# The first stage of a hybrid decoder layer: ones products ahead of the input, a compact weight block spread on chip, and squares behind the splits

## The chip, the cores and the metric

The kernel runs on one core of one Trainium2 chip. The metric is the device time of one execution in microseconds (us); the median of three runs is compared. A second number, the span, is taken from one profiled execution: it runs from the first to the last instruction that the profiler recorded.

## The reference

One layer (`DEPTH = 1`) of a decoder trunk, batch 1, 512 tokens behind 16 meta tokens, so 528 positions of 1024 channels, all in float32:

```
h = concat(meta, x)                       # 528 x 1024
u = rmsnorm(h) * mix_norm_w
proj = u @ w_in                           # pool 1024 | z 2048 | xbc 4096 | dt 32 | gates 2048
y_pool = pool_mixer(proj.pool) @ w_pool_up
y_ssd  = mamba2(z, xbc, dt) @ w_ssd_out   # conv + silu, chunked SSD, gated group norm
h = h + (sigmoid(g0) * y_pool + sigmoid(g1) * y_ssd) @ w_o
h = h + relu(rmsnorm(h) @ w_ff1)**2 @ w_ff2
out = rmsnorm(h)[16:]
```

In the first stage three things are made from x: the 32 columns of dt (one for each head), the first columns of xbc, and the mean of the squares of each position, from which the norm's factor `rsb = 1/sqrt(mean + eps)` comes. The factor is applied after the products here, so that they need not wait for it.

## The kernel before, in words

**Split products.** TensorE multiplies in a rounded float32 format (FP32R). For accuracy every operand is split in two: `hi` is the value cast to FP32R, and `lo` is what is left. ScalarE (ACT) makes `hi`, VectorE (DVE) subtracts it to make `lo`, and a product is three passes: hi·hi (L140), lo of the data with hi of the weights (L141), and hi of the data with lo of the weights (L143). `proj_step` writes these three for one slice k of 128 input channels, for each of two column runs of a result; `proj` runs it over k = 0 to 7.

**Weights.** All weights lie in DRAM as blocks of 128 x 1024. A block is loaded into `raw` (3 buffers, L68, from the queue of SyncE), cast into `whi` (4 buffers, L69, ACT) and split into `wlo` (4 buffers, L70, DVE). A `whi` buffer comes free only when the products of the block four before it have read it. Block 0 is dt, block 1 the first B columns (the result `px0_16`), block 2 the C columns (`px0_24`), blocks 3 and 4 two x blocks (`px0_0`, `px0_1`), 5 and 6 the two z blocks (one result, `pz0`), 7 to 9 gates (`pgp`).

**First stage** (L172 to L194). dt has only 32 columns. Its block holds them four times side by side, so that each quarter of the 128 result rows has all heads, and each quarter is later used for another stretch of 128 tokens. For k = 0 to 7 the slice `xt[k]` is loaded (L179), ACT scales and casts it to `xh[k]` (L180), DVE makes `xl[k]` (L181), TensorE runs two `proj_step` (dt into `pdt`, B into `px0_16`, 12 products in all), and ACT squares `xt[k]` (L190 and L193) with DVE adding the squares up in `q` (L194; the squares have 2 buffers). The two weight blocks come in an early part of 256 columns (slices 0 and 1) and a late part of 768.

**Norm factor.** `q` is split (L200, L201), four products with a matrix of ones sum it over the partitions (L209, L210, result `pn`), ACT takes the root (L211) and DVE the reciprocal (L212): `rsb`.

**The rest of the first group.** `px0_24`, `px0_0`, `px0_1` and `pz0` follow on TensorE. The wide results have two PSUM buffers that are taken in turn: `px0_16`, `px0_24`, `px0_0`, `px0_1`, `pz0`. So `px0_0` may begin when `px0_16` has been copied out, and `pz0` when `px0_0` has. The copy is `first_raw` (L295, ACT) into `raw0` (2 buffers), followed by a multiplication with `rsb` (L296, DVE), the convolution (L279 on ACT, three taps L282 on DVE) and a SiLU (L284, ACT). A `raw0` buffer comes free when its convolution is done.

**What sets the order.** The program is written as one sequence; the framework schedules it and decides in which order each engine takes its instructions. Each engine then runs its own list strictly in order, with semaphores between engines. So a line that moves in the source may move instructions of other lines too, on every engine.

Of the kernel before, what the change touches and what calls it, by code (L numbers as in the profile page):

```python
# [9 lines left out]
F32 = mybir.dt.float32  # L10
F32R = mybir.dt.float32r
AF = mybir.ActivationFunctionType
ALU = mybir.AluOpType

P = 128
# [5 lines left out]
NK = D // P  # L21
G = 8
R = 4
HEADS = 32
# [7 lines left out]
OFF_DT = 7168  # L32
# [7 lines left out]
GATES_FIRST = 3  # L40
GATE_AT = {1: 3, 2: 4, 3: 5, 5: 6}
POOL_ORDER = (3, 2, 1, 0)


@with_exitstack
def kernel(ctx: ExitStack, tc, xT, x, w, vec, fnw, out):
    nc = tc.nc
    act, dve, pe, pool = nc.scalar, nc.vector, nc.tensor, nc.gpsimd
# [10 lines left out]
    def block_tiles():  # L59
        b = nblk[0]  # L60
        nblk[0] += 1
        return (b, wp.tile([P, 1024], F32, tag="raw", name=f"raw{b}", bufs=3),
                wp.tile([P, 1024], F32R, tag="whi", name=f"whi{b}"),
                wp.tile([P, 1024], F32R, tag="wlo", name=f"wlo{b}"))

    def block_part(t, c):
        b, raw, hi, lo = t
        nc.sync.dma_start(raw[:, c], w[b, :, c])  # L68
        act.copy(hi[:, c], raw[:, c])  # L69
        dve.tensor_tensor(lo[:, c], raw[:, c], hi[:, c].bitcast(F32), op=ALU.subtract)  # L70

    def block():
        t = block_tiles()
        block_part(t, slice(0, 1024))
        return t[2:]
# [17 lines left out]
    ones_r = const.tile([P, P], F32R, name="ones_r")  # L93
# [14 lines left out]
    def col(off, i, n=P):  # L108
        return vs[:n, off + i : off + i + 1]
# [20 lines left out]
    def psum2(name):  # L130
        return psa.tile([P, 1024], F32, tag="mm", name=name)

    def psum1(name):
        return psb.tile([P, 512], F32, tag="s", name=name)

    def proj_step(outs, k, wblk, rhs):

        wh, wl = (t[:, k * P : (k + 1) * P] for t in wblk)
        for o, c in outs:
            pe.matmul(o, wh, rhs[0][k][:, c], start=k == 0, stop=False)  # L140
            pe.matmul(o, wh, rhs[1][k][:, c], start=False, stop=False)  # L141
        for o, c in outs:
            pe.matmul(o, wl, rhs[0][k][:, c], start=False, stop=k == NK - 1)  # L143
# [5 lines left out]
    def wide(ps, skip=0):  # L149

        h = (L - skip) // 2
        runs = [(ps[:, 512 - h : 512], slice(skip, skip + h)),
                (ps[:, 512 : 512 + h], slice(skip + h, L))]
        return runs, ps[:, 512 - h : 512 + h]
# [11 lines left out]
    X, U = (xh, xl), (uh, ul)  # L166
# [3 lines left out]
    pdt = [psum1(f"pdt{i}") for i in range(2)]  # L170
    dt_runs = [(pdt[0][:, : NM + 256], slice(0, NM + 256)), (pdt[1][:, :256], slice(NM + 256, L))]
    pB = psum2("px0_16")  # L172
    runsB, viewB = wide(pB)
    wdt, wB = block_tiles(), block_tiles()
    early, late = slice(0, 256), slice(256, 1024)
    for k in range(NK):
        if k == 0:
            block_part(wdt, early)
        nc.sync.dma_start(xt[k], xT[:, k, :])  # L179
        act.activation(xh[k], xt[k], AF.Copy, scale=col(V_MIX, k))  # L180
        dve.scalar_tensor_tensor(xl[k], xt[k], col(V_MIX, k), xh[k].bitcast(F32),  # L181
                                 op0=ALU.mult, op1=ALU.subtract)
        if k < 2:
            block_part((wB, wdt)[k], (early, late)[k])
        if k == 1:
            block_part(wB, late)
        proj_step(dt_runs, k, wdt[2:], X)
        proj_step(runsB, k, wB[2:], X)
        if k == 0:
            act.activation(q, xt[k], AF.Square)  # L190
        else:
            s = pre.tile([P, L], F32, tag="sq", name=f"sq{k}", bufs=2)
            act.activation(s, xt[k], AF.Square)  # L193
            dve.tensor_tensor(q, q, s, op=ALU.add)  # L194
# [11 lines left out]
    for i in range(2):  # L206
        c = slice(i * HALF, (i + 1) * HALF)
# [37 lines left out]
    for c in (slice(0, P), slice(P, W)):  # L245
        n = c.stop - c.start
# [5 lines left out]
    for j, src in enumerate((dt, acs)):  # L252
# [6 lines left out]
              start=True, stop=True)  # L259
# [302 lines left out]
    def gate_ssd(d):  # L562
        ps = psum1(f"pgs{d}")
        proj(narrow(ps), block(), U)
        gt = gtp.tile([P, SEQ], F32, tag="gt", name=f"gs{d}")
        act.activation(gt, ps, AF.Sigmoid, bias=col(V_BG, NK + d))
        return gt

    wgb = block()
    pend = [pool_tile(2 * POOL_ORDER[0] + i) for i in range(2)]  # L570
    for n, gi in enumerate(POOL_ORDER):
        nxt = []
        if n < 3:
            nxt.append(pool_tile(2 * POOL_ORDER[n + 1]))
        if n == 0:
# [6 lines left out]
        if n < 3:  # L582
            nxt.append(pool_tile(2 * POOL_ORDER[n + 1] + 1))
        pend = nxt


    gts.append(gate_ssd(1))
    ks = [2 * gi + i for gi in POOL_ORDER for i in range(2)]
    for d in range(NK):
        ps = psum2(f"pup{d}")[:, :SEQ]  # L590
        wh, wl = block()
        for n, k in enumerate(ks):
            c = slice(k * P, (k + 1) * P)
# [8 lines left out]
    for d in range(NK):  # L602
# [8 lines left out]
        h = mgp.tile([P, SEQ], F32R, name=f"mh{d}")  # L611
# [17 lines left out]
    for half in range(2):  # L629
# [5 lines left out]
        for kk in range(4):  # L635
            wh, wl = block()
            for k2 in range(2):
                k = 2 * kk + k2
                c = slice(k2 * 512, (k2 + 1) * 512)
# [4 lines left out]
        c = slice(half * 512, (half + 1) * 512)  # L644
        for t in range(4):
            dve.tensor_tensor(ht[:, t, c], ht[:, t, c], pv[t], op=ALU.add)
        for kk in range(4):
            k = 4 * half + kk
# [179 lines left out]
    c = NC - 1  # L828
# [5 lines left out]
    for t in range(4):  # L834
        T, st = t // 2, slice((t % 2) * P, (t % 2 + 1) * P)
        n = 0
        for half in range(2):
            parts = [(0, 512)] if half == 0 or t < 3 else [(0, 256), (256, 256)]
            for a, m in parts:
# [4 lines left out]
                for k, seg in ((1, (A11, 3)[T]), (0, (A12, A22)[T])):  # L844
                    wh, wl = wq[k, half]
                    for p in range(2):
# [3 lines left out]
                        for lhs, rhs in ((hh, wh), (hh, wl), (hl, wh)):  # L850
                            pe.matmul(ps, lhs[:, p, seg, st], rhs[:, x0 : x0 + m], start=f and lhs is hh and rhs is wh,
                                      stop=i == 4 and lhs is hl, skip_group_check=True)
# [11 lines left out]
def _weight_blocks(i):  # L864

    w_in, w_g, w_up = i["w_in"][0], i["pool_w_group"][0], i["w_pool_up"][0]
    w_so, w_o, f1, f2 = i["w_ssd_out"][0], i["w_o"][0], i["w_ff1"][0], i["w_ff2"][0]
    blocks = []

    def cols(m, c):  # L870
        a = m[:, c : c + P]
        return a.reshape(NK, P, P).transpose(1, 0, 2).reshape(P, NK * P)

    def put(b):
        blocks.append(b)

    put(cols(np.tile(w_in[:, OFF_DT : OFF_DT + HEADS], (1, P // HEADS)), 0))

    def group(g, gate_d=None):
        for t in (16 + g, 24 + g, 2 * g, 2 * g + 1):  # L880
            put(cols(w_in, OFF_XBC + t * P))
        if gate_d is not None:
            gate(gate_d)
        for j in range(2):
            put(cols(w_in, OFF_Z + (2 * g + j) * P))

    def wg(b):
        put(w_g[2 * b : 2 * b + 2].reshape(2, 2, P, 256).transpose(2, 0, 1, 3).reshape(P, 1024))

    def gate(d):  # L890
        put(cols(w_in, OFF_GATE + d * P))

    def pieces(ks):

        u = [w_so[k * P : (k + 1) * P, d * P : (d + 1) * P] for d in range(NK) for k in ks]
        return [np.concatenate(u[j : j + NK], 1) for j in range(0, len(u), NK)]

    group(0)
    for d in range(GATES_FIRST):
        gate(d)  # L900
    for g in range(G - 1):
        if g == 4:
            for d in range(NK):
                put(cols(w_so[:D], d * P))
        group(g + 1, GATE_AT.get(g))
    blocks += pieces(range(8, 14))
    wg(POOL_ORDER[0] // 2)
    for t in range(2):
        put(cols(w_in, (2 * POOL_ORDER[0] + t) * P))
    for n in range(4):  # L910
        if n < 3:
            put(cols(w_in, 2 * POOL_ORDER[n + 1] * P))
        if n == 0:
            gate(NK - 1)
        if n == 3:
            gate(NK)
        if n == 2:
            wg(POOL_ORDER[n] // 2)
        if n < 3:
            put(cols(w_in, (2 * POOL_ORDER[n + 1] + 1) * P))  # L920
    gate(NK + 1)
    for d in range(NK):
        put(cols(w_up, d * P))
    last = pieces((14, 15))
    for d in range(NK):
        if d + 2 < NK:
            gate(NK + d + 2)
        if d % 4 == 0:
            put(last[d // 4])

    def rows(m, k2, half):
        a = m[k2 * 2 * P : (k2 + 1) * 2 * P, half * 512 : (half + 1) * 512]
        return a.reshape(2, P, 512).transpose(1, 0, 2).reshape(P, 1024)

    for half in range(2):
        for kk in range(4):
            put(rows(w_o, kk, half))

    def quarter(c, k, half):

        a = [f2[(4 * c + 2 * p + k) * P : (4 * c + 2 * p + k + 1) * P, half * 512 : (half + 1) * 512]
             for p in range(2)]
        return np.concatenate(a, 1)

    def quarters(c):
        for k, half in ((1, 0), (1, 1), (0, 1), (0, 0)):
            put(quarter(c, k, half))

    ff = list(range(32))

    def ff1():
        if ff:
            put(cols(f1, ff.pop(0) * P))

    for _ in range(6):
        ff1()
    for c in range(8):
        quarters(c)
        for _ in range(3 if c > 4 else 4):
            ff1()  # L960
    return np.ascontiguousarray(np.stack(blocks))
# [38 lines left out]
```

## Time and profile before

| | us |
|---|---|
| median of three runs | 1034.2 (1033.74 to 1035.4) |
| the profiled execution, its own time | 1033.66 |
| its span | 1031.9 |
| TensorE (PE) busy | 1017.8, 99% |
| VectorE (DVE) busy | 714.5, 69% |
| ScalarE (ACT) busy | 542.5, 53% |

The span is 1.8 us shorter than the execution's own time. Times within the trace count from the span's start. A row of the timeline gives the start, the duration, the engine, the line, the operation with output and inputs, the shape and, in brackets, how long the engine was idle before it and what ended that. "x2" merges neighbours of one kind. PE durations are modelled to the end of the pipeline, so that neighbours overlap: the distance of two starts is the rate.

### The profile page before, as it was taken

To read this page: it belongs to the slowest core of one execution; us is meant where nothing else is said; L and a number is where in the kernel's file an instruction comes from. 1 tells how busy PE (TensorE), PEld (TensorE's weight loads), DVE (VectorE), ACT (ScalarE), POOL (GpSimd) and SP (SyncE) were. 2 spreads that over 40 slices of the span, in tenths; PEclk is the share of its full clock that TensorE was granted. 3 is DMA by queue.
4 is the path that set the end of the run, shared out by engine and by line. 5 is a ranking of instruction groups with operands and counts; after the bars stand their busy time and mean duration, and the time that the engine had idled before them with its cause. 6 is when DMAs were issued, how large, how long until landed. Compare 5 with 4: busy or idle time off the path is not lost.

```text
span 1031.9 us, 13993 instructions
## 1 busy us (share of the span) xinstructions
PE 1017.8 (99%) x5700; PEld 880.1 (85%) x5700; DVE 714.5 (69%) x932; ACT 542.5 (53%) x706; POOL 10.0 (1%) x24
## 2 busy tenths in 40 slices
PE   7999999999999999999999999999999999999997
PEld 7889989998889898988998888878888888888886
DVE  7978788687637586887674345645686676776866
ACT  8675968586627348573443223344554355454444
POOL 0100000000000000000000000000000000000000
PEclk9999999999999999999999999999999999999999
DMA  6333051413332321413232323543324323334112
GB/s 228 115 137 103 21 164 39 146 57 127 102 111 75 108 97 41 151 61 113 72 109 89 102 84 102 202 145 108 95 82 123 105 80 121 102 102 123 42 41 82
DMA packets 29424, 106.01 MB, mean 103 GB/s; under 512 B 3312, under 2 KB 4272, under 8 KB 28336
## 3 DMA queue, kind: packets, MB, share of 16 engines
q1 hardware_dynamic: 26640, 93.14, 28.6%
q0 software_dynamic: 2000, 11.08, 2.8%
q8 instruction: 45, 0.74, 0.3%
q10 hardware_dynamic: 720, 0.91, 0.2%
q14 instruction: 19, 0.16, 0.0%
HBM read 102.95 MB, written 2.16 MB: 102 GB/s over the span
## 4 chain that ended last, share of the span: by engine, by line
PE 97%; DVE 1%; DMA 1%; ACT 0%; issue 0%; SPq 0%; ACTq 0%
PE px L140 6%; PE px L141 6%; PE px L143 6%; PE pf L86 6%; PE pf L88 6%; PE pf L87 6%; PE alpha L744 3%; PE alpha L746 3%; PE alpha L745 3%; PE pz L140 3%; PE pz L141 3%; PE pz L143 3%; PE py L418 2%; PE pp L141 2%; PE pso L86 2%; PE pp L140 2%
## 5 line engine op out<-in xcount | busy, mean ns | idle before, releaser
L69 ACT CAST whi<-raw 128x1024 fp32r<-128x1024 f32 (+2 forms) x141 | 145.6, 1038 | 274.6 <-PE pf L87 61.2
L70 DVE TENSOR_TENSOR wlo<-raw,whi 128x1024 fp32r<-128x1024 f32 (+2 forms) x141 | 170.0, 1207 | 151.4 <-ACT whi L69 144.0
L140 PE MATMUL px<-uh,whi 128*128 128x264 f32 (+1 forms) x448 | 121.2, 290 | 0.7 <-DVE ct L282 0.7
L141 PE MATMUL px<-ul,whi 128*128 128x264 f32 (+1 forms) x448 | 118.9, 285 | 0.0
L86 PE MATMUL pf<-vh,whi 128*128 128x512 f32 x256 | 99.7, 389 | 1.2 <-DVE vl L653 1.2
L88 PE MATMUL pf<-vh,wlo 128*128 128x512 f32 x256 | 99.6, 389 | 0.0
L87 PE MATMUL pf<-vl,whi 128*128 128x512 f32 x256 | 99.6, 389 | 0.0
L143 PE MATMUL px<-uh,wlo 128*128 128x264 f32 (+1 forms) x448 | 90.8, 284 | 0.0
L140 PEld LDWEIGHTS px<-uh,whi 128*128 128x128 f32 x448 | 84.6, 189 | 2.8 <-issue 2.6
L141 PEld LDWEIGHTS px<-ul,whi 128*128 128x128 f32 x448 | 84.9, 189 | 0.3
L143 PEld LDWEIGHTS px<-uh,wlo 128*128 128x128 f32 x448 | 69.4, 188 | 0.3 <-issue 0.3
L695 DVE TENSOR_TENSOR slo<-b,shi 128x1024 fp32r<-128x1024 f32 x35 | 42.8, 1222 | 31.6 <-ACT shi L694 31.6
L694 ACT CAST shi<-b 128x1024 fp32r<-128x1024 f32 x35 | 36.8, 1051 | 51.8 <-PE pf L87 36.5
L86 PEld LDWEIGHTS pf<-vh,whi 128*128 128x128 f32 x256 | 48.0, 188 | 11.3 <-DVE vl L653 1.5
L88 PEld LDWEIGHTS pf<-vh,wlo 128*128 128x128 f32 x256 | 48.0, 188 | 10.1
L87 PEld LDWEIGHTS pf<-vl,whi 128*128 128x128 f32 x256 | 48.1, 188 | 10.0
L744 PE MATMUL alpha<-shi,hh 128*128 128x512 f32 x140 | 54.6, 390 | 0.0
L746 PE MATMUL alpha<-shi,hl 128*128 128x512 f32 x140 | 54.5, 389 | 0.0
L745 PE MATMUL alpha<-slo,hh 128*128 128x512 f32 x140 | 54.5, 389 | 0.0
L756 DVE TENSOR_TENSOR ht<-ht,alpha 128x1024 f32<-128x1024 f32 x35 | 42.6, 1218 | 6.1 <-PE alpha L746 6.1
L140 PE MATMUL pz<-uh,whi 128*128 128x512 f32 x112 | 44.0, 393 | 0.0
L141 PE MATMUL pz<-ul,whi 128*128 128x512 f32 x112 | 43.9, 392 | 0.0
(330 smaller groups left out, 2395.9 us busy)
## 6 DMA issues: line engine op xcount, KB each, us to landing
raw<-in_w SPq DMA_DIRECT2D x137, 512.0 KB, 3.6
b<-in_w SPq DMA_DIRECT2D x28, 512.0 KB, 3.6
abc<-acs_d POOLq DMA_DIRECT2D x8, 1024.0 KB, 7.2
xt<-in_xT SPq DMA_DIRECT2D x8, 264.0 KB, 6.2
ht<-in_x POOLq DMA_DIRECT2D x4, 512.0 KB, 5.8
w<-in_w SPq DMA_DIRECT2D x4, 512.0 KB, 3.5
out_dram<-out SPq DMA_DIRECT2D x4, 320.0 KB, 2.4
raw<-in_w SPq DMA_DIRECT2D x2, 384.0 KB, 5.5
```

Of the source, the lines that this page charges most:

```text
L69: act.copy(hi[:, c], raw[:, c])
L70: dve.tensor_tensor(lo[:, c], raw[:, c], hi[:, c].bitcast(F32), op=ALU.subtract)
L86: pe.matmul(ps, ah, bh, start=first, stop=False)
L87: pe.matmul(ps, ah, bl, start=False, stop=False)
L88: pe.matmul(ps, al, bh, start=False, stop=last)
L140: pe.matmul(o, wh, rhs[0][k][:, c], start=k == 0, stop=False)
L141: pe.matmul(o, wh, rhs[1][k][:, c], start=False, stop=False)
L143: pe.matmul(o, wl, rhs[0][k][:, c], start=False, stop=k == NK - 1)
L695: dve.tensor_tensor(lo, src, hi.bitcast(F32), op=ALU.subtract)
L744: pe.matmul(ps[t], a[0], wh[:, cs], start=f, stop=False, skip_group_check=True)
L745: pe.matmul(ps[t], a[0], wl[:, cs], start=False, stop=False, skip_group_check=True)
L746: pe.matmul(ps[t], a[1], wh[:, cs], start=False, stop=l, skip_group_check=True)
```

## The change

- Ahead of everything, TensorE runs 22 products of the 128 x 128 matrix of ones with itself into the buffer of `pdt[1]`, which the first real product overwrites.
- The dt block holds each weight once: 256 of its 1024 columns are used, [slice k][head]. They come in one load; ACT and DVE read them with a repeated (stride 0) access and write the four copies into `whi` and `wlo`, slices 0 and 1 first, the other six later. The late load of dt (768 columns) is gone.
- The loads stand in another order: `xt[2]` is asked for before the late part of block 1.
- The squares and their sums stand in a loop of their own, behind the splits and products of all eight slices.

```diff
+WARM = 22
...
     wdt, wB = block_tiles(), block_tiles()
-    early, late = slice(0, 256), slice(256, 1024)
-    for k in range(NK):
-        if k == 0:
-            block_part(wdt, early)
+    b, raw, hi, lo = wdt
+    nc.sync.dma_start(raw[:, :256], w[b, :, :256])
+    spread = lambda t: t.rearrange("p (k c h) -> p k c h", c=4, h=HEADS)
+    once = raw[:, :256].rearrange("p (k h) -> p k h", h=HEADS).unsqueeze(2).to_broadcast([P, NK, 4, HEADS])
+
+    for n in range(WARM):
+        pe.matmul(pdt[1][:, :P], ones_r, ones_r, start=True, stop=True)
+
+    def x_load(k):
         nc.sync.dma_start(xt[k], xT[:, k, :])
+
+    def x_split(k):
         act.activation(xh[k], xt[k], AF.Copy, scale=col(V_MIX, k))
         dve.scalar_tensor_tensor(xl[k], xt[k], col(V_MIX, k), xh[k].bitcast(F32),
                                  op0=ALU.mult, op1=ALU.subtract)
-        if k < 2:
-            block_part((wB, wdt)[k], (early, late)[k])
-        if k == 1:
-            block_part(wB, late)
+
+    x_load(0)
+    act.copy(spread(hi)[:, :2], once[:, :2])
+    dve.tensor_tensor(spread(lo)[:, :2], once[:, :2], spread(hi)[:, :2].bitcast(F32), op=ALU.subtract)
+    x_split(0)
+    block_part(wB, slice(0, 256))
+    x_load(1)
+    proj_step(dt_runs, 0, wdt[2:], X)
+    proj_step(runsB, 0, wB[2:], X)
+    x_split(1)
+    act.copy(spread(hi)[:, 2:], once[:, 2:])
+    dve.tensor_tensor(spread(lo)[:, 2:], once[:, 2:], spread(hi)[:, 2:].bitcast(F32), op=ALU.subtract)
+    x_load(2)
+    block_part(wB, slice(256, 1024))
+    proj_step(dt_runs, 1, wdt[2:], X)
+    proj_step(runsB, 1, wB[2:], X)
+    for k in range(2, NK):
+        if k > 2:
+            x_load(k)
+        x_split(k)
         proj_step(dt_runs, k, wdt[2:], X)
         proj_step(runsB, k, wB[2:], X)
+    for k in range(NK):
         if k == 0:
             act.activation(q, xt[k], AF.Square)
...
-    put(cols(np.tile(w_in[:, OFF_DT : OFF_DT + HEADS], (1, P // HEADS)), 0))
+    wdt = w_in[:, OFF_DT : OFF_DT + HEADS].reshape(NK, P, HEADS).transpose(1, 0, 2).reshape(P, NK * HEADS)
+    put(np.concatenate([wdt, np.zeros((P, 1024 - NK * HEADS), wdt.dtype)], 1))
```

The built order of the changed program differs from before on every engine up to about the end of the first group's z product, and is the same from there on. Three places of it: On ACT the squares of k = 3 to 7 and the split of `q` now stand among the casts of blocks 2 to 5. On DVE the splits of blocks 3, 4 and 5 now stand ahead of the `lo` half of `q`. And on ACT the cast of block 8 (`whi8`), which waits for the last hi product of `px0_1`, now stands ahead of the SiLU of B and of the copy of `px0_0`; before it stood behind that copy.

## The prediction

> **What bounds the kernel now.** I read the page first, then the waits of PE, the stretches, and the timeline of each engine over the first 40 us.
>
> ```profile
> span 1031.9 us, 13993 instructions
> ...
> PE 1017.8 (99%) x5700; PEld 880.1 (85%) x5700; DVE 714.5 (69%) x932; ACT 542.5 (53%) x706; POOL 10.0 (1%) x24
> ```
> ```profile
> PE pf L86 <- DVE vl L653: 1.2, 1, 1.2
> PE px L140 <- DVE ct L282: 0.7, 1, 0.7
> ```
> ```profile
> 20.79:38.87 18.08, 18.08 (x151) 18.05 (x149) 17.95 (x31) 13.85 (x20) 0.00 (x0) 1.00 0.40 117
> ```
>
> PE is busy for 99% of the span: whatever PE loses or gains in the first stage reaches the end unless a later wait of PE swallows it, and after the start the waits of PE hold these two entries and one of 0.6. The stretch row (PE, PEld, DVE, ACT, POOL in turn) says that from 20.79 to 38.87 PE has no gap, but DVE has none either (17.95 of 18.08). So work put later on DVE stays late. Now the first stage itself.
>
> ```profile
> 5.46 0.81 PE L140 MATMUL pdt<-xh,whi 128*128 128x272 f32 x2 [5.46 <-ACT xh L180]
> ...
> 8.60 0.43 PE L140 MATMUL pdt<-xh,whi 128*128 128x272 f32 x1
> 8.82 0.43 PE L141 MATMUL pdt<-xl,whi 128*128 128x272 f32 x1
> ...
> 9.91 0.28 PE L141 MATMUL px<-xl,whi 128*128 128x264 f32 x1
> 10.03 0.28 PE L140 MATMUL px<-xh,whi 128*128 128x264 f32 x1
> ...
> 12.27 0.51 PE L141 MATMUL pdt<-xl,whi 128*128 128x272 f32 x2 [0.61 <-DVE xl L181]
> ...
> 20.79 0.41 PE L209 MATMUL pn<-qhn,ones_r 128*128 128x264 f32 x2
> ```
>
> PE starts at 5.46. Until about 9.7 products start 0.22 us apart, afterwards 0.12: half speed at first. At 12.27 PE gets `xl[2]`, then runs without a gap: 9 products left of k = 2 and 60 of k = 3 to 7 lie before 20.79, so 8.52 / 69 = 0.1235 us each. All 96 at that rate would need 11.9 us, so the stage ends 20.79 - 5.46 - 11.9 = 3.4 us later than full speed from the same start would allow. That is the most that can be won there.
>
> **The change, part by part. The gain.** What gates PE is the chain of splits.
>
> ```profile
> 6.99 0.74 ACT L180 ACTIVATE xh<-xt,vs 128x528 fp32r<-128x528 f32 x1 [0.27 <-DMA xt<-in_xT]
> 7.95 0.83 ACT L69 CAST whi<-raw 128x768 fp32r<-128x768 f32 x1 [0.22 <-DMA raw<-in_w]
> 8.97 0.83 ACT L69 CAST whi<-raw 128x768 fp32r<-128x768 f32 x1 [0.19 <-DMA raw<-in_w]
> 9.71 0.64 ACT L193 ACTIVATE sq<-xt 128x528 f32<-128x528 f32 x1
> 10.26 0.72 ACT L180 ACTIVATE xh<-xt,vs 128x528 fp32r<-128x528 f32 x1
> 10.88 0.63 ACT L193 ACTIVATE sq<-xt 128x528 f32<-128x528 f32 x1
> ```
> ```profile
> 7.76 0.77 DVE L181 SCALAR_TENSOR_TENSOR xl<-xt,vs,xh 128x528 fp32r<-128x528 f32 x1 [1.13 <-ACT xh L180]
> ...
> 8.81 0.96 DVE L70 TENSOR_TENSOR wlo<-raw,whi 128x768 fp32r<-128x768 f32 x1 [0.28 <-ACT whi L69]
> ...
> 9.69 0.22 DVE L101 COPY sel<-ident 128x128 f32<-128x128 f32 x1
> ...
> 9.83 0.22 DVE L102 COPY sel<-ident 128x128 f32<-128x128 f32 x1
> ...
> 11.45 0.77 DVE L181 SCALAR_TENSOR_TENSOR xl<-xt,vs,xh 128x528 fp32r<-128x528 f32 x1
> ...
> 12.13 0.70 DVE L194 TENSOR_TENSOR q<-q,sq 128x528 f32<-128x528 f32 x1
> ```
>
> From start to start: on ACT `xh` 0.62, a 768 cast 0.74; on DVE `xl` 0.68, a 768 split 0.88, a `sel` copy 0.14. The first four loads are the same, so `xh[1]` stays at 6.99 and `xl[1]` at 7.76. The 768 cast of dt no longer waits for a load: ACT 7.62 to 8.45, DVE from 8.48. Then DVE does `xl[2]` at 9.36, the two `sel` at 10.05, the 768 split of B at 10.33 (its cast runs on ACT from about 9.0 to 9.8, its load is the sixth in the queue, as that of the row at 8.97 was, with `xt[2]` of 264 KB ahead of it in place of 384 KB, so it lands no later) and `xl[3]` from 11.21 to 11.98. PE has k = 0 to 2 behind it by then (the last two products of k = 2 wait for that split until about 11.3) and takes `xl[3]` at 12.03. 59 products are left: 12.03 + 59 x 0.1235 = 19.32. Later `xl` come every 0.68 while PE needs 12 x 0.1235 = 1.48 for a slice. **Gain: 20.79 - 19.32 = 1.47.** The stride 0 reading has no row; it moves the same number of elements, so I take the same time (a half faster to a half slower on the 768 pair would be 0.4 either way, as the pair's DVE half lies on the chain).
>
> The ones products cost nothing if they end before `xl[0]` is there: `xh[0]` releases PE at 5.46, the split takes 0.77 more, about 6.2; PE has one product to run before it.
>
> ```profile
> 1.10 0.35 DVE L96 CAST ones_r<-ones_f 128x128 fp32r<-128x128 f32 x1
> ...
> 75.64 1.05 PE L390 MATMUL pcb<-ct,bt 128*128 128x128 f32 x8
> ```
>
> They start at 1.5. The nearest rows of that shape are eight passes of plain float32: (1.05 - 0.28) / 7 = 0.11 us apart at full speed, so 0.22 at half speed, 22 x 0.22 = 4.8, end 6.3: hidden. If each needed two passes, as the float32 ones do (four products, eight rows), it is the rival below. What they bring is small: without them PE would be at half speed until 9.67 as now, k = 0 and 1 would take until 10.6, k = 2 until 12.1, and the stage would end at 19.5, 0.15 later. [...]
>
> The missing load (384 KB) and its queue slot free loads that nothing waits for. The squares cost ACT and DVE the same; only their place changes.
>
> **The price.** The squares and splits of `q` come later, and with them `rsb`.
>
> ```profile
> 19.23 1.22 DVE L70 TENSOR_TENSOR wlo<-raw,whi 128x1024 fp32r<-128x1024 f32 x1
> 19.36 0.63 ACT L200 CAST qhn<-q 128x528 fp32r<-128x528 f32 x1
> ...
> 20.37 0.71 DVE L201 TENSOR_TENSOR qln<-q,qhn 128x528 fp32r<-128x528 f32 x1
> ...
> 33.16 0.67 DVE L282 SCALAR_TENSOR_TENSOR bt<-raw,vs,bt 128x525 f32<-128x525 f32 x1
> ```
>
> Three more splits of 1.13 to 1.22 stand ahead of `ql`, on an engine without gaps: its end moves from 21.08 to about 24.4. PE wants it after 40 products of `px0_24` and two of `pn`, 19.32 + 42 x 0.121 = 24.4. No slack: I charge 0.1, up to 0.7.
>
> Worse is ACT's order. `pz0` needs the copy of `px0_0`; ahead of it in ACT's list now stand the cast of block 8, a table load and the SiLU of B, and the cast of block 8 may not begin before PE's last hi product of `px0_1`, two products ahead of `pz0`. The same four ran in this order once before, with another block:
>
> ```profile
> 32.95 1.05 ACT L69 CAST whi<-raw 128x1024 fp32r<-128x1024 f32 x1 [0.90 <-PE px L141]
> 34.02 1.28 ACT L284 ACT_TABLE_LOAD   x1
> 35.32 0.65 ACT L284 ACTIVATE bt<-bt 128x528 f32<-128x528 f32 x1
> 35.87 0.58 ACT L295 COPY raw<-px 128x528 f32<-128x528 f32 x1
> ...
> 38.82 1.06 ACT L69 CAST whi<-raw 128x1024 fp32r<-128x1024 f32 x1 [0.71 <-PE px L141]
> ```
> ```profile
> 38.87 0.39 PE L140 MATMUL pz<-xh,whi 128*128 128x512 f32 x1
> ```
>
> 32.95 to 36.45 is 3.50 us. In the trace of before the block 8 cast was released at 38.82, 0.05 before `pz` started. So PE, which could start `pz0` at 38.87 - 1.47 + 0.1 = 37.5, waits for it until 3.5 later: **3.5 lost**, on PE, with nothing beside it. The table load also waits for the third tap of B: 33.83 before, now 3.3 later with `ql` and one more split of 1.2 ahead of it, 38.3, against the cast's end at 38.5. So the cast decides; each us by which the tap is later would be added. Behind `pz0` the dt transposes stand a few products later in PE's list; I charge 0.1.
>
> Sum: -1.47 + 0.1 + 3.5 + 0.1 = **+2.2 us**. Against the profiled execution, 1031.9 span and 1033.66 own time, that is 1034.1 and 1035.9; that execution is 0.5 below the median of 1034.2, so the median forecast is **1036.4**. The unknown costs (gain 1.0 to 1.9, `ql` 0 to 0.7, the tap up to 0.5, transposes 0 to 0.1) give +1.6 to +3.8, 1035.8 to 1038.0.
>
> **Rivals.** *Swallowed later, not slower.* PE's later waits, 0.7 for `ct` above and one of 1.2 for `vl`, could shrink by as much as PE comes late, if what they wait for does not move.
>
> ```profile
> 128.15 0.79 ACT ct L279
> ```
>
> Then 1.9 is given back: 1034.5, and with the gain at its bound of 3.4 even 1032.6. It decides where DVE's work ahead of those waits does not hang on PE. Against it: on the chain of waits the `ct` piece begins with ACT at 128.15, right behind PE's last product of that result, so it moves with PE. Chance 0.12.
>
> *The clock falls in the hole.*
>
> ```profile
> 1025.84 0.28 PE L851 MATMUL last<-shi,hl 128*128 128x256 f32 x1
> ```
> ```profile
> 1030.00:1030.50 0.50, 0.00 (x0) 0.00 (x0) 0.00 (x0) 0.00 (x0) 0.00 (x0) 0.69 0.93 344
> ```
>
> PE's last product starts at 1025.84, and the granted clock (0.69 in this half microsecond, 1.00 up to it) falls some 4.3 us later. Had it fallen in the hole of 3.5, PE would restart at half speed for about as long as at the start (5.46 to 9.7) and lose half of 4.2: 1036.4 + 2.1 = 1038.5. The rows speak against it, since 3.5 is under 4.3, but a moment earlier or later in the clock's own rhythm isn't excluded. Chance 0.09. [...]
>
> *The ones products hold PE up.* With two passes each they need 0.44 at half speed: 9.5 of them in 4.2 us, the other 12.5 at 0.22 in 2.75, end at 8.5. PE then needs 96 x 0.1235 = 11.86 and is done at 20.35, the gain is 0.44, the time 1034.2 + 3.7 - 0.4 = 1037.5. If the clock stays low all the while they end at 11.2, the stage at 23.1, 2.3 later than before: 1034.2 + 2.3 + 3.7 = 1040.2. It decides from an end later than about 7.5, when `xl[3]` no longer sets the stage. Chance 0.09.
>
> That the change doesn't do what it says, I don't see: the built program has the ones products, the single load and the late squares.
>
> **How the numbers follow.** About 0.2% (2.07 us) is what a measurement of this kernel can tell from no change. The forecast, 2.2 within 1.6 to 3.8, has 0.70, and lies just past that line: 0.44 of it slower, 0.26 within. The swallowed case gives 0.07 within and 0.05 faster. The two last rivals, 0.18, are slower. Slower 0.62, same 0.33, faster 0.05. The range takes in the forecast's bounds and reaches to the near ends of the rivals: from 1034.5 (swallowed) to 1038.7 (the clock, the first ones case); what lies outside is half the swallowed case and the long ones case, 0.10 to 0.15. The forecast's own range is 1035.8 to 1038.0.
>
> **What would show it.** In the profile after: the 0.12 us rate from about 6 us on; `xl[3]` at 11.2 on DVE and its first product at 12.0; the first product of `px0_24` at 19.3; `ql` ending about 24.4 with PE at it; the block 8 cast on ACT at 37.5, and behind it table load, SiLU, copy and `pz` at 41.0, with a wait of PE for ACT's copy of about 3.5 in its list; then PE without a gap, 2.1 behind before. I am wrong if `pz` starts without a wait, if PE takes `xl[3]` after 13, if the waits of 0.7 and 1.2 shrink, or if behind the hole the products of `pz` start twice as far apart as in the trace of before.

## The result, and the profile after

The changed kernel takes 1037.74 us (median of six runs, 1037.36 to 1038.3), the kernel before, in the same runs, 1033.67 (six runs, 1032.97 to 1035.4): a ratio of 1.0037 with a 95% interval of 1.0027 to 1.0047. It is slower by 4.1 us. The profiled execution after took 1037.66 with a span of 1036.0, against a span of 1031.9 before.

First the page of the changed kernel (busy time of each engine and its share of the span), then the waits of PE (engine, tile, line, what ended the wait; total, times, longest).

```profile
span 1036.0 us, 14035 instructions
...
PE 1023.3 (99%) x5722; PEld 885.9 (86%) x5722; DVE 715.0 (69%) x932; ACT 542.0 (52%) x706; POOL 10.0 (1%) x24
```
```profile
PE pz L141 <- ACT raw L321: 3.3, 1, 3.3
PE pdt L183 <- DVE ones_r L97: 1.5, 1, 1.5
PE pf L87 <- DVE vl L679: 1.2, 1, 1.2
PE px L141 <- DVE ct L308: 0.7, 1, 0.7
```

The 99% of PE tells nothing: it was 99% before too, and the 22 ones products count in it. The list of waits tells the case. The first entry is new and is the wait of `pz0` for the copy of `px0_0`. The second is only the time until the ones products start. The last two are those of before, to the tenth.

Now the timeline of PE at the start: the ones products, the first real products, the place where the rate changes, and the first product of `px0_24`.

```profile
1.51 4.96 PE L183 MATMUL pdt<-ones_r 128*128 128x128 f32 x22 [1.51 <-DVE ones_r L97]
6.26 0.54 PE L141 MATMUL pdt<-xh,whi 128*128 128x272 f32 x1
6.59 0.43 PE L142 MATMUL pdt<-xl,whi 128*128 128x272 f32 x1
6.82 0.41 PE L141 MATMUL pdt<-xh,whi 128*128 128x256 f32 x1
...
10.33 0.33 PE L141 MATMUL px<-xh,whi 128*128 128x264 f32 x1
10.49 0.28 PE L142 MATMUL px<-xl,whi 128*128 128x264 f32 x1
10.61 0.29 PE L141 MATMUL px<-xh,whi 128*128 128x264 f32 x1
...
19.88 0.29 PE L141 MATMUL px<-xh,whi 128*128 128x258 f32 x1
```

The ones lie (6.26 - 1.51) / 22 = 0.216 us apart. Behind them the real products still start 0.22 apart until 10.3, and only then 0.12. PE has no gap from 1.51 on, and yet full speed comes 0.7 later than before (9.7). The stage ends at 19.88 and not at 20.79: 0.91 won (in one profiled execution of each kernel).

The same stretch on DVE, where the splits that were to set the pace stand:

```profile
10.38 3.48 DVE L190 SCALAR_TENSOR_TENSOR xl<-xt,vs,xh 128x528 fp32r<-128x528 f32 x5
...
23.90 0.70 DVE L227 TENSOR_TENSOR qln<-q,qhn 128x528 fp32r<-128x528 f32 x1
```

`xl[3]` to `xl[7]` come in one row from 10.38, so `xl[3]` is there at about 11.1. PE's first product with it starts at 12.69. The splits are ahead of PE. Here PE at half speed sets the end of the stage, not DVE.

Then the hole ahead of `pz`: ACT, DVE and PE, one fence for each engine.

```profile
37.86 1.04 ACT L70 CAST whi<-raw 128x1024 fp32r<-128x1024 f32 x1 [1.76 <-PE px L142]
38.92 1.28 ACT L310 ACT_TABLE_LOAD   x1
40.22 0.64 ACT L310 ACTIVATE bt<-bt 128x528 f32<-128x528 f32 x1
40.77 0.58 ACT L321 COPY raw<-px 128x528 f32<-128x528 f32 x1
```
```profile
37.88 0.76 DVE L308 SCALAR_TENSOR_TENSOR bt<-raw,vs,bt 128x525 f32<-128x525 f32 x1
```
```profile
37.66 0.40 PE L144 MATMUL px<-xh,wlo 128*128 128x264 f32 x2
41.40 0.80 PE L141 MATMUL pz<-xh,whi 128*128 128x512 f32 x1 [3.33 <-ACT raw L321]
41.99 0.63 PE L142 MATMUL pz<-xl,whi 128*128 128x512 f32 x1
42.42 0.63 PE L144 MATMUL pz<-xh,wlo 128*128 128x512 f32 x1
...
44.55 0.40 PE L142 MATMUL pz<-xl,whi 128*128 128x512 f32 x1
44.78 0.39 PE L144 MATMUL pz<-xh,wlo 128*128 128x512 f32 x1
```

The cast of block 8 ends at 38.90, the table load follows at 38.92, and `pz` starts at 41.40 where it started at 38.87 before: 2.5 later, in spite of the 0.9 won. The third tap of B ends at 38.64, only 0.26 ahead of the cast's end. And behind the hole `pz` runs 0.43 apart until 44.55 and 0.23 afterwards. The stretches (PE, PEld, DVE, ACT, POOL busy, then the granted clock) say why:

```profile
38.10:41.00 2.90, 0.00 (x0) 0.00 (x0) 2.90 (x7) 2.87 (x4) 0.00 (x0) 1.00 0.01 6
41.00:41.40 0.40, 0.00 (x0) 0.00 (x0) 0.40 (x3) 0.40 (x2) 0.00 (x0) 0.66 0.00 0
41.40:44.50 3.10, 3.10 (x7) 2.48 (x8) 3.10 (x8) 1.69 (x3) 0.00 (x0) 0.50 0.01 4
44.60:48.00 3.40, 3.40 (x16) 2.77 (x15) 3.40 (x8) 0.65 (x1) 0.00 (x0) 1.00 0.49 152
```

The granted clock fell just before the hole ended and came back 3.4 us later. From the start of `pz` to the first product of `pgp` it is 14.08 us (41.40 to 55.48), against 12.70 before (38.87 to 51.57): 1.4 lost. The balance: -0.9 in the first stage; +3.4 for the hole (before, `pz` started 18.08 behind the end of the first stage, which would be 37.96 here, and it starts at 41.40); +1.4 for the clock. That is 3.9 together, and `px1`, the first result of the next group, does start 3.9 later (73.61 for 69.71). Another 0.2 of the 4.1 in the span comes later, from nothing that the waits show.

### The profile page after: what moved, and what is told of

It reads as the page before. It is cut to its first block, busy times and chain, and to the rows that moved or that the text cites. A ratio compares the mean times of both kernels' runs of the same rounds, so it can differ in the third digit from the quotient of the medians.

```text
span 1036.0 us, 14035 instructions
## 1 busy us (share of the span) xinstructions
PE 1023.3 (99%) x5722; PEld 885.9 (86%) x5722; DVE 715.0 (69%) x932; ACT 542.0 (52%) x706; POOL 10.0 (1%) x24
## 4 chain that ended last, share of the span: by engine, by line
PE 97%; DVE 1%; ACT 1%; issue 0%; ACTq 0%
PE px L141 6%; PE px L142 6%; PE px L144 6%; PE pf L87 6%; PE pf L89 6%; PE pf L88 6%; PE alpha L770 3%; PE alpha L772 3%; PE alpha L771 3%; PE pz L141 3%; PE pz L144 3%; PE pz L142 3%; PE py L444 2%; PE pp L142 2%; PE pso L87 2%; PE pp L141 2%
## 5 line engine op out<-in xcount | busy, mean ns | idle before, releaser
L70 ACT CAST whi<-raw 128x1024 fp32r<-128x1024 f32 (+1 forms) x139 | 144.1, 1043 | 271.4 <-PE pf L88 61.2
L71 DVE TENSOR_TENSOR wlo<-raw,whi 128x1024 fp32r<-128x1024 f32 (+1 forms) x139 | 168.5, 1213 | 150.7 <-ACT whi L70 143.4
L782 DVE TENSOR_TENSOR ht<-ht,alpha 128x1024 f32<-128x1024 f32 x35 | 42.5, 1214 | 6.1 <-PE alpha L772 6.1
```

## The experiments

**Squares back inside the loop.** All else of the change stays. In the built order ACT then has the copy of `px0_0` ahead of the cast of block 8 again.

```diff
+    def x_square(k):
+        if k == 0:
+            act.activation(q, xt[k], AF.Square)
+        else:
+            s = pre.tile([P, L], F32, tag="sq", name=f"sq{k}", bufs=2)
+            act.activation(s, xt[k], AF.Square)
+            dve.tensor_tensor(q, q, s, op=ALU.add)
...
         proj_step(runsB, k, wB[2:], X)
+        x_square(k)
-    for k in range(NK):
-        if k == 0:
...
```

> The changed kernel with only the squares and their sums put back into the loop over k; ones products, compact dt block and order of loads stay. In its built order the cast of block 8 stands behind the copy of px0_0 again. Theory (the loss is ACT's order, made by the late squares): PE's wait for that copy (3.3) and the half speed behind it (1.55) go; about 1037.7 - 4.9 = 1032.8, pz starts without a wait. Rival (the ones products or the stride 0 reading cost the time): the wait may go, but the time stays at 1035 or more because the first stage is late.

Measured: 1033.0 against 1033.7, ratio 0.9994 (0.9985 to 1.0004). No wait for the copy is left; `pz` starts at 38.12, without a gap. So the whole price comes from the squares' place and what it does to the order of other work. The first stage ends at 20.14: 0.65 won in this profiled execution.

**Squares behind alone**, in the kernel before (neither ones, nor one load of dt, nor the other order of loads).

```diff
         proj_step(runsB, k, wB[2:], X)
+    for k in range(NK):
         if k == 0:
             act.activation(q, xt[k], AF.Square)
```

> The kernel of before with one edit: squares and sums behind the eight slices. Theory: this edit alone brings the hole; PE waits some 3.3 to 3.6 for the copy of px0_0, and the clock may fall in it for one stretch of 3.4, which costs 1.5 more: before + 3.3 to 5.1, less what the first stage gains by DVE and ACT being free of the squares (up to 0.8): 1036.2 to 1038.8. Rival (the loss is made by the other edits): within 0.7 of before.

Measured: 1040.08 against 1033.7, ratio 1.0062 (1.0047 to 1.0077). The cause is right, the size was missed by over a microsecond.

```profile
PE pz L140 <- ACT raw L296: 3.9, 1, 3.9
```
```profile
38.68 1.04 ACT L69 CAST whi<-raw 128x1024 fp32r<-128x1024 f32 x1 [2.87 <-PE px L141]
39.74 1.28 ACT L285 ACT_TABLE_LOAD   x1
41.04 0.64 ACT L285 ACTIVATE bt<-bt 128x528 f32<-128x528 f32 x1
41.59 0.61 ACT L285 ACTIVATE ct<-ct 128x512 f32<-128x512 f32 x1
42.10 1.08 ACT L296 COPY raw<-px 128x528 f32<-128x528 f32 x2
```

Between the SiLU of B and the copy the built order here has the SiLU of C as well (0.5 from start to start), so the hole is 0.6 longer, and the clock falls here too. From `pz` to `pgp` it takes 14.39 us. Here the whole low stretch (43.51 to 46.93 by the granted clock) lies behind the start of `pz` at 42.74; in the run with 16 ones products below it does too (39.25 to 42.66, `pz` at 38.83), and there the same way takes 14.27. So all but about 0.1 of what exceeds the 12.70 of before is the clock. This profiled execution took 1039.2, the least of the four; the other three had a mean granted clock of 0.995 against its 0.998, so they probably lost more to the clock than the trace shows.

**The hole filled.** The changed kernel, with 14 more products between `px0_1` and `pz0` that write a PSUM tile nobody reads afterwards.

```diff
+        if first:
+            for n in range(14):
+                pe.matmul(pn[:, :512], ones_r, xh[n % NK][:, NM:], start=True, stop=True)
         ps = psum2(f"pz{g}")
```

> The changed kernel with 14 extra products of 512 columns between px0_1 and pz0 on PE; they write sums that nothing reads and fill most of the hole (14 x 0.233 = 3.3). Theory (the clock falls because PE stands idle): pz starts at the same time, 41.4, but its products follow at 0.23 from the first on; 1.55 less, 1036.2. Rival (the slow products behind the hole have another cause, such as ACT and DVE reading the same memory): pz still at 0.43, time 1037.7.

Measured: 1036.26 against 1033.7, ratio 1.0028 (1.0017 to 1.0038): 1.5 less than the changed kernel, though PE has 3.4 us more work.

```profile
39.03 3.43 PE L343 MATMUL pn<-xh,ones_r 128*128 128x512 f32 x14
42.53 0.50 PE L141 MATMUL pz<-xh,whi 128*128 128x512 f32 x1
42.87 0.40 PE L142 MATMUL pz<-xl,whi 128*128 128x512 f32 x1
43.10 0.39 PE L144 MATMUL pz<-xh,wlo 128*128 128x512 f32 x1
```

The products of `pz` start 0.23 apart from the second on, and `pz` to `pgp` takes 12.67 as before. The hole's second price is the clock, and it is about 1.4. (In this profiled execution the first stage ended 1.1 later than in that of the changed kernel, 21.0 for 19.9, which is why `pz` stands at 42.5. The sources of the two agree up to there, so a few tenths between the stage ends of two single profiles say little.)

**No ones products**, all else as changed.

```diff
-WARM = 22
+WARM = 0
```

> The changed kernel without the ones products. Theory (they release no clock and only hold PE until 6.26): PE starts at 5.4, full speed from 9.5 to 9.7, first product of px0_24 at about 19.4 instead of 19.88; hole and half speed as in the changed kernel; 0.4 less, 1037.3. Rival (the ones products do bring full speed earlier than without them): first product of px0_24 after 19.9, time 1037.7 or more.

Measured: 1039.06 against 1033.7, ratio 1.0055 (1.0038 to 1.0071): a miss, 1.8 above the 1037.3 expected. The first stage ends at 19.78, 0.1 earlier than with the ones; full speed comes at 11.2. And the built order moved with the ones: the SiLU of C again stands ahead of the copy, the wait is 3.9, the clock falls. What the ones do to the time of the changed kernel can't be read from this pair. So the same pair was run with the squares inside, where there is no hole:

> The changed kernel without the ones products and with the squares inside: what is left is the compact dt block and the order of loads. Theory (these two alone make the gain of the first stage, the ones nothing): PE starts at 5.3, no wait for the copy of px0_0, pz at 38.0 to 38.4, time 1033.0 as with the ones. Rival (the ones make the gain): pz at 38.8 as before, 1033.7.

Measured: 1033.01, ratio 0.9991 (0.9981 to 1.0), against 1033.0 with the ones: nothing. The first stage ends at 19.77 without them and at 20.14 with them, in one profile each. And the ones alone, added to the kernel before:

> The kernel of before with the 22 ones products of 128 columns alone. Theory (they hold PE until 6.26 and release nothing): the first real product 0.8 later than before, full speed 4 to 6 us behind it, 0.3 to 0.8 lost or, where the clock's rhythm falls well, nothing: 1033.7 to 1034.5, no hole. Rival (they bring full speed earlier): 1033.2 or less.

Measured: 1033.85 against 1033.94, ratio 0.9997 (0.9987 to 1.0006), first stage 20.93 (20.79 before). Full speed begins at 10.6. The 22 products of 128 columns bring nothing.

**Ones products of 256 columns**, squares inside.

```diff
+    ones_w = const.tile([P, 2, P], F32R, name="ones_w")
+    dve.tensor_copy(ones_w, ones_f.unsqueeze(1).to_broadcast([P, 2, P]))
...
-        pe.matmul(pdt[1][:, :P], ones_r, ones_r, start=True, stop=True)
+        pe.matmul(pdt[1][:, :256], ones_r, ones_w.rearrange("p a b -> p (a b)"), start=True, stop=True)
```

> As the run with the squares inside, but each of the 22 ones products has 256 columns instead of 128 (a second constant tile of 128 x 256 ones). In the runs so far full speed began 4.1 to 6.0 us after the first real product, with and without ones products, 8.9 to 10.7 us after the first ones product. Theory (a product of 128 columns keeps PE's array busy for half of the 0.225 us between two starts only, and that is too little): with 256 columns the ones count, full speed begins by 8.5 at the latest, products of the first slice are 0.12 apart from then on; the stage ends about 19.5 instead of 20.1, time 1032.4. Rival (constant data or a product into an unread buffer does not count): full speed again 4 to 6 us after the first real product, time 1033.0.

```profile
1.82 4.93 PE L185 MATMUL pdt<-ones_w,ones_r 128*128 128x256 f32 x22 [1.82 <-DVE ones_w L99]
6.59 0.41 PE L143 MATMUL pdt<-xh,whi 128*128 128x272 f32 x2
6.84 0.29 PE L143 MATMUL px<-xh,whi 128*128 128x264 f32 x1
6.97 0.41 PE L144 MATMUL pdt<-xl,whi 128*128 128x272 f32 x2
```

The same number of ones products in the same 4.8 us, and the first real products now start 0.12 apart. So it is neither the constant data nor the time for which PE runs that kept the clock down, but the width: with 128 columns, squares inside, the real products were 0.22 apart until 10.8. (Nor is it the chance of one profile: see the five kernels of each kind in the last section.) The time is 1033.05, ratio 0.9994 (0.9984 to 1.0003), the same as with 128 columns: PE gets its clock and then waits for `xh[2]` and `xl[2]` (0.6 and 0.5 in its list), with the stage's end at 19.97. With the squares inside, the splits set the pace.

**Both together: squares behind and 256 columns.** Now neither clock nor squares are in the way of the first stage.

> The changed kernel with ones products of 256 columns in place of 128; everything else stays, the squares behind the splits and ACT's order around the cast of block 8 too. Theory (products of 128 columns release no clock, so in the changed kernel the first stage is bound by PE at half speed and not by the splits): products 0.12 us apart from about 6.6, first product of px0_24 at 18.5 to 19.0 (19.88 with 128 columns; the forecast's 1.47 or more is reached), and the hole ahead of pz stays at 3.3 to 3.5. Time: 1 us less than the changed kernel, 1036.6 if the clock falls in the hole again, 1035.2 if not. Rival (the splits on DVE and ACT bound the stage anyway): px0_24 not before 19.6, time within 0.3 of the changed kernel or, without a fall of the clock, 1036.2.

Measured: 1038.23 against 1033.87, ratio 1.0042 (1.003 to 1.0055). Half of the expectation held: `px0_24` starts and the first stage ends at 18.46, 2.3 earlier than the stage ended before (20.79). The other half fell: `pz` starts at 41.59, no sooner than in the changed kernel.

```profile
36.73 1.05 ACT L70 CAST whi<-raw 128x1024 fp32r<-128x1024 f32 x1 [0.37 <-PE px L144]
39.11 1.28 ACT L312 ACT_TABLE_LOAD   x1 [1.34 <-DVE bt L310]
40.40 0.64 ACT L312 ACTIVATE bt<-bt 128x528 f32<-128x528 f32 x1
40.95 0.58 ACT L323 COPY raw<-px 128x528 f32<-128x528 f32 x1
```
```profile
38.27 0.76 DVE L310 SCALAR_TENSOR_TENSOR bt<-raw,vs,bt 128x525 f32<-128x525 f32 x1
```
```profile
41.59 0.79 PE L143 MATMUL pz<-xh,whi 128*128 128x512 f32 x1 [4.65 <-ACT raw L323]
```

The cast is done at 37.78, and the table load now waits 1.34 more for the third tap of B. So the hole has two bounds: the cast of block 8, and the tap, which hangs on the sums, `rsb` and a DVE without gaps. In the changed kernel they lie 0.26 apart. Whatever the first stage wins beyond that goes into a longer wait. The longer hole costs more clock as well: the clock is low from 40.23 to 47.06, and `pz` to `pgp` takes 15.22.

**Squares two slices behind**, 256 columns. The square of slice k - 2 stands in step k. In the built order the copy stands ahead of the cast of block 8.

```diff
         proj_step(runsB, k, wB[2:], X)
+        x_square(k - 2)
+    for k in range(NK - 2, NK):
+        x_square(k)
```

> Ones products of 256 columns, and the square of slice k-2 in step k (the last two behind the loop), so that the squares neither stand ahead of the first splits nor all come at the end; in the built order the copy of px0_0 stands ahead of the cast of block 8 on ACT. Theory (only that order makes the hole; the first stage is bound by xl[3] once PE has its clock): no wait of PE for the copy, first product of px0_24 at about 19.4 (20.21 with the squares in their old place and the same ones products), time 1033.05 - 0.8 = 1032.2. Rival (late squares as such hold PE up, through the sums and rsb, wherever the cast stands): a wait of PE of 1 us or more between px0_24 and pz, time 1033.5 or above.

Measured: 1033.72 against 1033.87, ratio 1.0 (0.9991 to 1.0009). The first stage ends at 18.95, 1.8 won, more than expected, and nothing of it reaches the end. The theory that only the order around the cast makes the hole falls here; the rival was right.

```profile
36.27 1.28 ACT L319 ACT_TABLE_LOAD   x1 [1.82 <-DVE bt L317]
37.57 0.64 ACT L319 ACTIVATE bt<-bt 128x528 f32<-128x528 f32 x1
38.12 0.58 ACT L330 COPY raw<-px 128x528 f32<-128x528 f32 x1
38.59 1.05 ACT L70 CAST whi<-raw 128x1024 fp32r<-128x1024 f32 x1
```
```profile
PE pz L143 <- ACT raw L330: 1.6, 1, 1.6
```

The cast of block 8 (38.59) is out of the way; the table load waits for the tap, and `pz` starts at 38.75, where it started before the change. In both this kernel and the last, `pz` comes 2.56 behind the tap's end (36.19 and 39.03): table load, SiLU, copy.

**The same with 16 ones products**, which end at 5.3.

> The same as the kernel two slices behind, with 16 ones products of 256 columns in place of 22: they end at about 5.3, close to where the first split is there, and not at 6.6. Theory (the real products go on with what the ones products began, and the stage is bound by xl[3]): first product of px0_24 within 0.2 of the kernel with 22, time the same within 0.3, 1032.2. Rival (with fewer ones the clock is released one period later): half speed up to about 10, px0_24 0.3 to 0.9 later, 1032.5 to 1033.1.

Measured: 1034.83 against 1033.87, ratio 1.0005 (0.9996 to 1.0014). Neither case came. Full speed is there from about 6.1 at the latest, the first stage ends at 18.54, 0.4 earlier than with 22 (one profile each), and the gain goes into a longer wait once more: `pz` at 38.83, a wait of 2.0. In the profiled execution the clock falls here, at 39.25, when PE has been at work again for 0.4:

```profile
39.20:42.00 2.80, 2.80 (x8) 2.21 (x7) 2.80 (x6) 2.26 (x4) 0.00 (x0) 0.51 0.00 0
```

`pz` to the dt transposes takes 7.01, against 5.47 in the kernel with 22, whose wait was 1.6 and whose clock held: 1.5 lost. It could also explain the times, if it does not happen in each execution: four of the 11 runs lie at 1033.1 to 1033.9, seven at 1034.8 to 1035.4. That the seven are those in which the clock fell is not shown: one of them was profiled, and the kernel with 22 has runs at 1034.9 to 1035.4 as well (three of 11), the kernel before, in the same series, at 1035.1 and 1035.3 (two of 21).

**The sums taken off DVE.** If DVE is the second bound, its seven additions might go to GpSimd, which is idle. First in the changed kernel, then with the squares inside and 256 columns.

```diff
-            dve.tensor_tensor(q, q, s, op=ALU.add)
+            nc.gpsimd.tensor_tensor(q, q, s, op=ALU.add)
```

> The changed kernel with its seven additions of squares on GpSimd in place of VectorE; ones products, loads and the squares' place stay. In the built order the copy of px0_0 now stands ahead of the cast of block 8. Theory (what is won in the first stage is given back at pz because the sums on VectorE push the third tap of B, and with it table load, SiLU and copy, some 4.8 us later than before): VectorE has 4.9 us less to do, the tap comes before 36, PE does not wait for the copy, pz starts 17.8 behind px0_24, at 37.7 (41.4 in the changed kernel), time 1033.7 - 1.1 = 1032.6. Rival (GpSimd's additions are slow, or slow VectorE's down): the sums end behind 24, the tap behind 37 and pz waits as before, 1035 or above.

Measured: 1040.43, ratio 1.0059 (1.0046 to 1.0073).

> Squares in their old place inside the loop, their additions on GpSimd, and ones products of 256 columns. Theory (with the clock released by 6.6 and nothing but splits on VectorE, PE runs the first stage without a gap, and the sums are early enough for pz not to wait): px0_24 at 18.5 to 18.9, pz at 36.3 to 36.7, no wait for the copy, time 1033.7 - 2.3 = 1031.4. Rival (the squares on ScalarE delay the casts and splits of x, as they did with the sums on VectorE): px0_24 at 19.8 or later, 1032.6 to 1033.1.

Measured: 1036.99, ratio 1.0027 (1.0016 to 1.0039). Both worse. In the first the sums end at 27.2 and PE waits 4.9 for the split of `q` in the middle of `px0_24`. In the second the first stage ends at 22.95, and the rows of the two engines are these:

```profile
10.76 10.30 DVE L192 SCALAR_TENSOR_TENSOR xl<-xt,vs,xh 128x528 fp32r<-128x528 f32 x6 [0.21 <-ACT xh L191]
```
```profile
10.19 12.04 POOL L201 TENSOR_TENSOR q<-q,sq 128x528 f32<-128x528 f32 x7 [8.57 <-ACT sq L200]
```

An addition takes GpSimd 12.04 / 7 = 1.72, and while it adds, a split takes DVE 10.30 / 6 = 1.72 as well, in place of 3.48 / 5 = 0.70 in the changed kernel. So the two take equally long side by side, 1.72 each; why, no run shows.

No kernel tried is clearly faster than the kernel before. The nearest are those with the squares inside, 1033.0 to 1033.05, 0.7 to 0.9 below the kernel before and 4.7 below the changed one; against before that is 0.1%, less than can be told here. Not run: the squares left behind, with the order of ACT or DVE itself changed, such as the taps ahead of the splits of later blocks.

## Why the prediction was right or wrong

The direction and the main step, the hole made by ACT's order, held. That the time also lies in the forecast's own range (1037.74 in 1035.8 to 1038.0) is in part luck: the gain came out below its bounds (1.0 to 1.9), and the clock fell, which the sum did not hold and a rival priced at 1038.5 did, with a chance of 0.09. One of the forecast's own signs of being wrong came true: behind the hole the products of `pz` start 0.43 apart, and 0.23 before. Step by step:

- **The gain, 1.47: mis-sized, it was 0.91.** The step that failed is that the splits gate PE. `xl[3]` was there at 11.1, not at 11.98, but PE ran at half speed until 10.3. With the clock there it comes to 1.47 and more: with 256 columns the stage ended at 18.46, 2.3 won.
- **The ones products: half right.** One pass each, 0.22 apart, end at 6.26, hidden: as worked out. That they release the clock at 6 was wrong: the 0.12 rate came at 10.3, though PE worked without a gap from 1.51 on. Nor were they worth 0.15: with the squares inside, the time was the same without them (1033.01 and 1033.0).
- **The `lo` half of `q`: right.** It ended at 24.60 and PE took it at 24.94, with no wait listed. The 0.1 charged was not needed.
- **The hole, 3.5, with cast, table load, SiLU and copy in that order: right.** `pz` at 41.40 for the 41.0 forecast, later by nearly what the gain fell short. The tap was at 38.64 (38.3) against the cast's end at 38.90 (38.5). That the tap was so near was said; what it means, that a larger gain would have bought nothing, was not, and the experiments with 256 columns show it.
- **The clock falls in the hole: it came, at 0.09.** It cost 1.4 where 2.1 was forecast: the low clock lasted 3.4 us, 0.3 of it still in the hole, and not 4.2, all of it behind. What failed is the reading of the row against it: that the clock fell 4.3 after the last product of the kernel shows one hole that was long enough, not the shortest that is. A wait of 3.33 took the clock here, and with 16 wide ones a wait of 2.0 did too, in one profile.
- **Swallowed later: did not come.** The waits of 0.7 and 1.2 are unchanged, as the argument on the `ct` piece had it.
- **The sum.** +2.2 was forecast and +4.1 came in the span: 0.6 for the gain, 1.4 for the clock, the 0.2 charged for `ql` and the transposes not needed, the rest unplaced. Both terms at fault hang on the clock. The upper end of the whole range, 1038.7, lies 0.2 above the 1038.5 of the rival it is said to come from; no term was given for the difference.

## What to carry to other kernels

When a step is taken out of the way of the first stage, ask what else hangs on it further down: here the sums fed `rsb`, the taps, a table load and a copy, and PE met that chain 20 us later. A gain ahead of such a meeting point goes into the wait there, so cost both ends of the wait and see how near the second bound lies. And a hole in PE's work is paid for twice if the granted clock falls in it (3.4 for the hole and 1.4 for the clock here); a few products that nobody needs can be cheaper than the idle hole (1036.26 against 1037.74 here).

## What the runs showed of the hardware

- 22 products with 128 columns of F32R, their weights loaded for each, took 4.75 us at half speed, and with 256 columns 4.77 us (4.86 where the clock stayed low to their end): the narrow ones were no faster. And in five kernels with the narrow ones the real products went over to full speed only 4.1 to 5.9 us behind them; in the five with the wide ones it came at the latest 1.3 us behind.
- After the hole of 3.3 us the clock was low for 3.41 us (41.12 to 44.54, by the granted clock of the changed kernel), in the filled hole it did not fall (products of `pz` 0.23 apart). In two other kernels it was low for 3.42 (squares behind alone) and 3.41 (16 wide ones), in the one with the wait of 4.65 for 6.83, twice that. In the changed kernel 30.72 us lie between the rise at 10.40 and the fall, nine times 3.41. No run was made to test what sets these lengths.
- Over the first 73 us the clock fell in six of the 14 traces, in each in a wait of PE of 2.0 us or more or less than a microsecond behind it: 2.0 with 16 wide ones, 3.3 in the changed kernel, 3.9 with the squares behind alone and with no ones, 4.65 with the squares behind and wide ones, 4.9 with the sums on GpSimd in the changed kernel (there the products behind it start 0.22 apart until 31.1). It held behind the wait of 1.6 two slices behind with 22 wide ones (products 0.23 apart), and behind the later ones of 0.7 and 1.2 before and after the change (granted clock 1.00). Between 1.6 and 2.0 nothing was measured.
- The stretches show a granted clock of 1.00 for the first microseconds of these kernels (1.00 from 6.26 to 10.40 in the changed one), while products start 0.22 apart. There the distance of starts is the better witness.
- While GpSimd added (1.72 us for 128x528), DVE took 1.72 for a split of 128x528, which takes it 0.70 in the changed kernel, where GpSimd does not add.
